# Low parts of 36 weight tiles made ahead, in the feed-forward stage, and kept in DRAM

## The chip, the cores and the metric

The kernel runs on one NeuronCore of a Trainium2 chip. The metric is the device time of one execution in microseconds, as the median of several runs. The engines go by short names: PE (TensorE matmul) and PEld (its weight loads), DVE (VectorE), ACT (ScalarE), POOL (GpSimd) and SP (SyncE, which here only issues DMAs).

## What is computed

Two transformer blocks in float32 on 512 tokens of 1024 features. The first has two mixers (a gated linear attention and a sliding-window attention) and a feed-forward part of 4096 hidden features. The second takes a vector `c` that modulates its norms, has two more mixers, and ends in a layer of 16384 single-neuron experts. What the change touches:

```python
# block 1, feed-forward
h = h + square(relu(f @ w_ff1)) @ w_ff2
# block 2, modulation
mod = silu(c) @ ada_w + ada_b                  # 6 x 1024 numbers
# block 2, experts, per token and head: the 16 best of 16384
s  = q @ sub_keys ; si = top_k(s, 16) ; eidx = si[0] * 128 + si[1]
act = gelu(x . u_tab[eidx]) ; y = sum(softmax(score) * act * v_tab[eidx])
```

## The kernel before, in words

**Products in two parts.** Every large product takes its float32 operands as a high part, rounded to the format in which PE is fast, and a low part, the rest. `split` (from line 287) makes both: ACT copies the high part, DVE or POOL subtracts it from the source. `chain` (line 327) then does three products per step: high x high (line 331), high x low (line 332) and, after all of these, low x high (line 334); the low part of the weights is needed last.

**Feed-forward stage (`ffn`, line 994).** Two halves of the hidden features (q = 0, 1). In each, 16 blocks of the first product, each ended by `ev` (relu on ACT, square on POOL, split on ACT and DVE), and then 16 steps of the second product. Weights come as 512 KB blocks on SP into four buffers (`weights`, line 296). Between these steps the generator `modulation` (line 501) is advanced: once per block of the first product, and 2 - q times per step of the second. A step of it issues the load of a 384 KB row block of `ada_w` on SP two steps ahead (line 523, three buffers) and adds one block to a sum on DVE (line 536). Every eighth step ends a sum: a transpose and a reduction on DVE (lines 542, 544) give `ap`, a small product on PE (line 546) adds over the partitions, and four small additions on DVE (`biased`, line 509) follow four steps later, once step KL = 3 of the next sum is through.

**The experts.** The first 128 tokens gather their experts' rows. For the other 384 tokens the first product is computed densely: 128 tiles of 128 experts each (`dense_S`, line 1570). A tile loads `ur` (512 KB, SP), makes `uh` (ACT, line 1575) and `ul` (line 1576), runs one chain of 24 matmuls, and applies gelu on ACT. `ur`, `uh` and `ul` have two buffers each. The first NSW = 59 tiles are made ahead of the second product, by `more_S`, while the routing runs; for these POOL makes `ul`, for the other 69 DVE does. The tiles beyond the sixth wait in DRAM (`Sd`).

**The routing** picks the experts. `topk_head` (line 1373) is a run of small DVE ops per head and token tile; `route_end` (line 1633) has PE transpose the numbers `ef`; `make` (line 1601) writes one-hot rows with DVE (`oh`, line 1612, and `ow`, line 1615, four buffers each), and `build` (line 1618) turns them into weights with PE (`gps`, line 1626). Per 16 tokens one `make`, one `topk_head` for the next tile, one `build` and 3, 2 or 1.5 tiles of `more_S` (for token tile 1, 2, 3) are written in this order.

**Order.** A planner orders each engine's instructions ahead of time, by the written order as priority and its own estimate of when operands are ready; each engine and each DMA queue then works through its list in order. `pin` puts an instruction behind the one written just before it on the same engine.

Of the kernel before, what the change touches and what calls it, by code (L numbers as in the profile page):

```python
# [9 lines left out]
F32 = mybir.dt.float32  # L10
# [11 lines left out]
KC = 8  # L22
# [13 lines left out]
NSW = 59  # L36
GBUF = 6
# [62 lines left out]
def layout(a):  # L100
    """the inputs in the order in which the kernel reads them: feature-major activations, weights in blocks of 128
    or 256 columns, one column per 128 entries of a vector"""
# [44 lines left out]
def tile_blocks(  # L147
# [26 lines left out]
    # ---------------------------------------------------------------- constants  # L174
# [72 lines left out]
    def small_constants():  # L247
        nc.scalar.dma_start(out=cf, in_=a["cf"])
        with tc.tile_pool(name="init", bufs=1) as ip:
# [4 lines left out]
            # sqrt(w^2 + eps) of the first block's last norm  # L254
# [28 lines left out]
    # ---------------------------------------------------------------- matrix products  # L283
# [12 lines left out]
    def weights(w, m, n, eng=None, step=None):  # L296
        """a block [128, m, n] of weights and its split, step of the m at a time"""
        if ready:
            return ready.pop(0)
        if raws:  # L300
            raw, step = raws.pop(0), W0
        else:
            raw = wtile(F32, "raw", RB, m, n)
            nc.sync.dma_start(out=raw, in_=w)
        hi = wtile(F32R, "whi", WB, m, n)
        lo = wtile(F32R, "wlo", WB, m, n)
        for k in range(0, m, step or m):
            ks = slice(k, k + (step or m))
            split(hi[:, ks], lo[:, ks], raw[:, ks], eng)
        return hi, lo, raw  # L310

    def ahead(w, hi, lo, eng=None, step=None):
        """a block of 128 columns split ahead of its turn, in other room than that of the weights"""
# [13 lines left out]
    def chain(ps, ab, first=True, last=True):  # L327
        """sum of a^T b over the pairs of split operands (a, b); a's low parts are needed last"""
# [7 lines left out]
    def gemm_fm(ws, X, N, evac, kouter=None, after=None, mid=None, eng=lambda s: None):  # L336
        """feature-major: evac(s, psum[128, N]) per block s of 128 columns; the first two blocks step by step together
        where kouter, the kind of their banks (their operand X is just coming in); after(s, raw weights);
        mid(k) after step k of these; eng(s): which engine makes the low parts of the weights"""
# [23 lines left out]
    def meta_fm(raw, um):  # L363
        """feature-major projection of the 16 meta tokens: psum[128, 16]"""
        ps = tr_tile("meta")
        for k in range(KC):
            PE.matmul(ps[:, 0:META], raw[:, k, :], um[:, k, :], start=(k == 0), stop=(k == KC - 1))
        return ps[:, 0:META]

    def gemm_tm(w, X, evac, after=None, n=256):  # L370
        """token-major: evac(b, psum[128 tokens, n]) for the n columns of w [128, KC, n]; one b per step"""
# [16 lines left out]
    def newton(ps, eps, n):  # L388
        """ps [128, n]: sums of D squares; -2 D / sqrt(ps / D + eps), its logarithm's estimate refined once"""
# [10 lines left out]
    def newton_small(ss, eps, n, tmp):  # L400
        """ss [128, m] SBUF: sums of n squares -> 1 / sqrt(ss / n + eps) in ss"""
# [8 lines left out]
    class SquareSum:  # L410
        """sums over the features of (x * wcol)^2: all chunks but the last are added up on the way"""
# [34 lines left out]
    def scaled_X(xr, wcol):  # L446
        """split of xr * wcol"""
# [5 lines left out]
    class Early:  # L453
        """two blocks of weights times X that still lacks the factor and the shift of its norm: flush(s) adds what the
        shift brings and evacuates"""
        def __init__(self, ws, X, cols, shift, evac, room, factor):
            """shift [128, KC]; room(s): two tiles of half a block's size; factor() makes the norm's factor"""
# [26 lines left out]
    def norm_X(X, xr, rs, wcol, bcol, keep=None):  # L484
        """split of xr * rs * wcol + bcol (wcol carries the factor of rs)"""
# [15 lines left out]
    def modulation(ip):  # L501
        """one step per call of next: rows of ada_w"""
# [6 lines left out]
        def biased(n, pm):  # L509
            o = VEC["ada_b_2"][0] + n * NM  # L510
            for e in range(4):
                es = slice(32 * e, 32 * e + 32)
                V.tensor_add(mod[es, n * NM:(n + 1) * NM], pm[es, 0:AW // 32].rearrange("p (m e) -> p m e", e=4)[:, :, e],
                             vec[es, o:o + NM])

# [12 lines left out]
        for n in range(6 * D // AW):  # L528
            am = ip.tile([128, AW], F32, name="am")
            for k in range(KC):  # L530
# [6 lines left out]
                if late and k == KL:  # L537
                    biased(*late.pop())
                yield
            # the sum over the partitions: 32 at a time by a transpose, the four of them by a product  # L540
# [4 lines left out]
            pm = tr_tile()  # L545
            PE.matmul(pm[:, 0:AW // 32], same32, ap, start=True, stop=True)
            late.append((n, pm))
        while late:
            biased(*late.pop())
# [8 lines left out]
    # ---------------------------------------------------------------- block 1  # L558
# [13 lines left out]
    def sigmoid(dst, src):  # L572
        """exp(-ln(1 + exp(-src))), src at least -43"""
# [4 lines left out]
    def gla(X, um, Y, sp, rs, rsT, hooks):  # L578
        """returns the parts in the order in which they may run; rs, rsT: factors of the columns and rows of products
        with X"""  # L580
# [35 lines left out]
        def decay():  # L616
            # decay: running sums of log sigmoid, restarted every 128 tokens
# [15 lines left out]
        def proj_v(h):  # L633
            """the values; with the first half of their columns, the 16 of the decay's first product"""
# [27 lines left out]
        def state():  # L662
            # state after the meta tokens
# [21 lines left out]
        def proj_r(i):  # L685
            """the gate of head i, into what it gates or in its place"""
# [17 lines left out]
        def within():  # L704
            """within a chunk: A^T[j, i], level by level, two chunks at a time; a level's factors are made a step ahead of its
            products"""
# [6 lines left out]
            def factors(n):  # L713
# [16 lines left out]
                # queries of the two heads of a pair side by side, each with zeros for the other's features  # L730
# [96 lines left out]
    def head_norm(po, eps, sp, rz=None):  # L827
        """token-major [128, 4 x 128] in PSUM -> rms normalised per head; rz: [128, 4] factors on po"""
# [17 lines left out]
    def swa(X, um, Y, sp, rs):  # L846
# [8 lines left out]
        # the rotated halves; all other rows stay zero  # L855
# [16 lines left out]
        def keys(ps, n, c0, rs=None):  # L872
            """the two kv heads, each then repeated on the other half of the partitions"""
# [89 lines left out]
    def out_proj(w, Yf):  # L963
        """half(kh, evac, pool): adds the products with half the rows of w, 256 columns per step"""
# [29 lines left out]
    def ffn(X, xr, rs, factor, step, done):  # L994
        """two halves of the hidden features: the first product's half stays on chip for the second; rs: the square
        of the factor of X's columns, made by factor()"""
        FH = DFF // NQ
        NS = FH // 128
        with stage("ffn") as sp:
            for q in range(NQ):  # L1000
                hh = sp.tile([128, NS, T], F32R, name="hh")
                hl = sp.tile([128, NS, T], F32R, name="hl")
                def ev(i, ps):
# [7 lines left out]
                    next(step)  # L1011
                gemm_fm(wrange(a["w_ff1"], q * NS, NS), X, T, ev, kouter="mm")
                for n2 in range(4):
                    pss = [bank("acc" if n2 % 2 else "sc", f"ff{e}") for e in range(2)]
                    for kq in range(NS // 4):
                        r0 = q * NS + kq * 4
                        for _ in range(2 - q):
                            next(step)
                        hi, lo, _ = weights(a["w_ff2"][n2, :, r0:r0 + 4, :], 4, 256)
# [17 lines left out]
    def block1():  # L1037
# [69 lines left out]
        with tc.tile_pool(name="ada", bufs=2) as ip:  # L1107
            step = modulation(ip)
            ffn(X, xr, rs2, factor, step, done)
# [3 lines left out]
    # ---------------------------------------------------------------- block 2  # L1113
    def mlstm(X, Y, sp, sums, wb):
# [4 lines left out]
        # gates  # L1119
# [137 lines left out]
    def diff(X, Y, sp, gates):  # L1257
        """gates(b, psum[128 tokens, 8]): the gates of the other mixer come with the first values"""
# [65 lines left out]
    def block2(xr, X, wb, sums):  # L1324
        """sums: what gives the factor of the final norm of the first block times that of the first norm here; X comes in
        without it and without the shift"""
# [38 lines left out]
    # ---------------------------------------------------------------- experts  # L1365
# [7 lines left out]
    def topk_head(h, s, sp, ef, fv):  # L1373
        """s [128, 2, 128]: scores of the two halves of head h -> expert numbers (float) and scores of its 16 best"""
# [7 lines left out]
        # sums of the ranks a, b: a, b >= 4 has 24 sums before it that are no less, so only a < 4 (at 16 a + b) and b < 4  # L1382
        # (at 4 a + 48 + b) are wanted
# [50 lines left out]
    with stage("h2") as sp:  # L1434
        xts = [sp.tile([128, D], F32, name=f"xt{b}") for b in range(NB)]

        def rows_of(dst, src, h, copy):
            """the 4 chunks h of src [128, KC, 128 tokens], token-major"""
# [34 lines left out]
    # ---------------------------------------------------------------- gathered tokens (the first 128)  # L1473
# [38 lines left out]
    # until the second product starts, the room for its operands takes gathered rows  # L1512
# [18 lines left out]
    def gather_step(n=1.0):  # L1531
        """issue the next n gathers; their use follows GLAG gathers later"""
# [9 lines left out]
    # ---------------------------------------------------------------- dense tokens: first product  # L1542
# [7 lines left out]
    def more_S(n):  # L1550
        """n further tiles ahead of the second product; those beyond LA wait in DRAM"""
# [18 lines left out]
    def dense_S(i, eng, tag, bufs):  # L1570
# [5 lines left out]
        eng.tensor_tensor(out=ul, in0=ur, in1=uh.bitcast(F32), op=OP.subtract)  # L1576
# [6 lines left out]
    # ---------------------------------------------------------------- routing; weight of every expert per dense token  # L1583
# [14 lines left out]
    with tc.tile_pool(name="rt", bufs=1) as sp:  # L1598
        made = []

        def make(b, n):
            """one-hot rows of the two halves of the expert number for 16 tokens n of tile b, one of them times the
            score in two parts of 12 bits (times GS: far from the least numbers of 16 bits)"""
# [14 lines left out]
        def build(b, n):  # L1618
            """the weights of 16 tokens n of tile b"""
# [106 lines left out]
    # ---------------------------------------------------------------- residual, last norm, out  # L1726
# [10 lines left out]
    def rows():  # L1737
        """the last norm's weight and the gate of the residual, the same row on all partitions"""
# [34 lines left out]
    # ---------------------------------------------------------------- dense tokens: second product  # L1773
# [8 lines left out]
    def load_G(k, p):  # L1782
        """part p of GP of the weights of 8 tiles"""
# [11 lines left out]
    for i in range(128):  # L1795
# [21 lines left out]
        # the last NL tiles together: the first tokens are complete while the others are still being added  # L1817
# [48 lines left out]
```

## Time and profile before

| what | value |
|---|---|
| median of 3 runs | 2322.53 us (2321.42 to 2325.12) |
| span of the profiled execution | 2316.9 us (its own time is not listed apart; the runs lie 4.5 to 8.2 us above the span) |
| PE busy | 2196.2 us, 95% |
| DVE busy | 1781.6 us, 77% |
| POOL busy | 1031.0 us, 44% |
| ACT busy | 903.7 us, 39% |

A busy share is an average over stages; the feed-forward stage lies between some 278 and 640 us, the routing between some 944 and 1436 us. "Granted clock" is PE's, as a share of full speed. An entry such as `ul<-ur,uh` names what an instruction writes and reads; L1576 is line 1576 of the kernel.

### The profile page before, as it was taken

What the parts mean: (1) busy time and instruction counts of PE and PEld (TensorE: products, weight loads), DVE (VectorE), ACT (ScalarE), POOL (GpSimd) and SP (SyncE); (2) the same over time, 40 slices, a digit from 0 to 9 for tenths busy, and PEclk for the clock granted to TensorE, in tenths of its full rate; (3) what the DMA queues carried; (4) which work ended last, traced back from release to release, by engine and by line L of the source; (5) the groups of instructions that cost most, each with busy time, mean ns of one, the idle gap of its engine ahead of it and who ended that gap; (6) DMA issues with size and microseconds to landing.
All of it is one profiled execution on the core that took longest, in us unless ns stands there. A gap on an engine that the chain in (4) does not pass through costs nothing.

```text
span 2316.9 us, 30890 instructions
## 1 busy us (share of the span) xinstructions
PE 2196.2 (95%) x11067; PEld 1865.7 (81%) x11067; DVE 1781.6 (77%) x3276; ACT 903.7 (39%) x1529; POOL 1031.0 (44%) x609
## 2 busy tenths in 40 slices
PE   9999999999989999997979999999999999999996
PEld 7777777877768777776969998776789999999994
DVE  5876657654485787899999965565679998989987
ACT  3345542233334664533334443333333333333333
POOL 1310221121150003512334434777788787778776
PEclk9999999999999999998989999999999999999998
DMA  5111357553222212631545667888889999999983
GB/s 178 59 39 46 118 161 244 179 168 106 81 92 78 64 61 85 227 98 62 186 135 189 212 222 238 285 264 281 273 316 327 338 336 322 340 339 330 340 305 136
DMA packets 181268, 455.09 MB, mean 196 GB/s; under 512 B 16597, under 2 KB 82006, under 8 KB 178042
## 3 DMA queue, kind: packets, MB, share of 16 engines
q1 hardware_dynamic: 82080, 252.58, 32.7%
q0 software_dynamic: 36864, 134.23, 16.2%
q10 hardware_dynamic: 62170, 66.30, 8.3%
q8 instruction: 87, 1.43, 0.3%
q14 instruction: 67, 0.55, 0.1%
HBM read 412.63 MB, written 39.79 MB: 195 GB/s over the span
## 4 chain that ended last, share of the span: by engine, by line
PE 42%; DVE 25%; issue 16%; POOL 9%; DMA 5%; ACT 2%; ACTq 0%; POOLq 0%; DVEq 0%; SPq 0%
PE do L1826 6%; POOL gt L1484 5%; PE mm L331 4%; PE mm L332 3%; PE mm L334 3%; POOL vl L1807 3%; PE S L331 3%; PE S L332 3%; PE S L334 3%; DVE oh L1612 3%; PE ff L331 2%; PE ff L334 2%; PE ff L332 2%; DVE ow L1615 2%; DVE vacc L1510 1%
## 5 line engine op out<-in xcount | busy, mean ns | idle before, releaser
L331 PE MATMUL S<-xhi,uh 128*128 128x384 f32 x1024 | 355.8, 347 | 5.9 <-ACT sg L1580 4.7
L332 PE MATMUL S<-xlo,uh 128*128 128x384 f32 x1024 | 352.4, 344 | 0.0
L1576 POOL TENSOR_TENSOR ul<-ur,uh 128x1024 fp32r<-128x1024 f32 x59 | 157.7, 2677 | 289.8 <-ACT uh L1575 208.6
L289 DVE TENSOR_TENSOR wlo<-raw,whi 128x1024 fp32r<-128x1024 f32 (+4 forms) x150 | 175.6, 1175 | 129.9 <-ACT whi L288 100.4
L1826 PE MATMUL do<-vh,wl 128*128 128x512 f32 x768 | 245.7, 399 | 15.2 <-DVE wl L1814 15.1
L1826 PE MATMUL do<-vl,wh 128*128 128x512 f32 x768 | 245.9, 400 | 10.9 <-POOL vl L1807 10.7
L1826 PE MATMUL do<-vh,wh 128*128 128x512 f32 x768 | 245.9, 400 | 1.1 <-ACT vh L1806 0.9
L1510 DVE SCALAR_TENSOR_TENSOR vacc<-gt,act,vacc 128x1024 f32<-128x1024 f32 x127 | 211.0, 1661 | 41.9 <-DMA gt<-in_v_dram,eidx 40.2
L288 ACT CAST whi<-raw 128x1024 fp32r<-128x1024 f32 (+4 forms) x152 | 146.1, 969 | 231.9 <-PE ff L332 107.2
L1492 DVE SCALAR_TENSOR_TENSOR gt<-gt,h2t 128x1024 f32<-128x1024 f32 x118 | 176.4, 1503 | 65.3 <-DMA gt<-in_u_dram,eidx 65.1
L331 PE MATMUL mm<-xhi,whi 128*128 128x512 f32 x544 | 219.8, 404 | 0.7 <-DVE xc L1127 0.7
L1575 ACT CAST uh<-ur 128x1024 fp32r<-128x1024 f32 x128 | 134.4, 1050 | 215.5 <-DMA ur<-in_ut_dram 115.0
L332 PE MATMUL mm<-xlo,whi 128*128 128x512 f32 x544 | 217.2, 399 | 0.0
L1807 POOL TENSOR_TENSOR vl<-vr,vh 128x1024 fp32r<-128x1024 f32 x64 | 174.8, 2732 | 80.7 <-ACT vh L1806 72.7
L331 PEld LDWEIGHTS S<-xhi,uh 128*128 128x128 f32 x1024 | 199.0, 194 | 9.5 <-ACT sg L1580 5.0
L332 PEld LDWEIGHTS S<-xlo,uh 128*128 128x128 f32 x1024 | 198.8, 194 | 3.2
L334 PE MATMUL S<-xhi,ul 128*128 128x384 f32 x1024 | 201.1, 339 | 0.0
L1807 POOL TENSOR_TENSOR vl<-vx,vh 128x1024 fp32r<-128x1024 f32 x64 | 169.3, 2645 | 61.5 <-ACT vh L1806 60.7
L1813 ACT CAST wh<-sg 128x384 fp32r<-128x384 f32 x128 | 65.5, 513 | 316.9 <-PE do L1826 210.1
L1826 PEld LDWEIGHTS do<-vh,wl 128*128 128x128 f32 x768 | 145.1, 190 | 53.6 <-DVE wl L1814 20.7
L1826 PEld LDWEIGHTS do<-vl,wh 128*128 128x128 f32 x768 | 145.7, 191 | 50.8 <-POOL vl L1807 17.0
L1484 POOL DMA_INDIRECT gt<-in_v_dram,eidx x128 | 166.7, 1303 | 32.5 <-issue 25.4
(481 smaller groups left out, 4819.8 us busy)
## 6 DMA issues: line engine op xcount, KB each, us to landing
ur<-in_ut_dram SPq DMA_DIRECT2D x128, 512.0 KB, 5.5
raw<-in_w_ff_dram SPq DMA_DIRECT2D x64, 512.0 KB, 3.6
vr<-in_v_dram SPq DMA_DIRECT2D x64, 512.0 KB, 4.6
vx<-in_v_dram SPq DMA_DIRECT2D x64, 512.0 KB, 7.6
aw<-in_ada_w_dram SPq DMA_DIRECT2D x64, 384.0 KB, 3.8
Gd<-gst ACTq DMA_DIRECT2D x24, 1024.0 KB, 4.3
gti<-Gd ACTq DMA_DIRECT2D x90, 256.0 KB, 5.0
raw<-in_w_in_dram SPq DMA_DIRECT2D x32, 512.0 KB, 4.4
```

Of the source, the lines that this page charges most:

```text
L288: S.copy(hi, src)
L289: (eng or V).tensor_tensor(out=lo, in0=src, in1=hi.bitcast(F32), op=OP.subtract)
L331: PE.matmul(ps, ah, bh, start=first and i == 0, stop=False, skip_group_check=True)
L332: PE.matmul(ps, ah, bl, start=False, stop=False, skip_group_check=True)
L334: PE.matmul(ps, al, bh, start=False, stop=last and i == n - 1, skip_group_check=True)
L1484: pin(G.indirect_dma_start(out=gt, out_offset=None, in_=tab, in_offset=bass.IndirectOffsetOnAxis(ap=eidx[:, s:s + 1], axis=0)))
L1492: ins = V.scalar_tensor_tensor(gt, gt, 1.0, h2t, op0=OP.mult, op1=OP.mult, accum_out=act[:, s:s + 1])
L1510: V.scalar_tensor_tensor(vacc, gt, act[:, s:s + 1], vacc, op0=OP.mult, op1=OP.add)
L1575: S.copy(uh, ur)
L1576: eng.tensor_tensor(out=ul, in0=ur, in1=uh.bitcast(F32), op=OP.subtract)
L1807: G.tensor_tensor(out=vl, in0=vr, in1=vh.bitcast(F32), op=OP.subtract)
L1826: PE.matmul(po[2 * tb + h], w[:, ts], v[:, h * 512:(h + 1) * 512], start=first and n == 0, stop=last and n == 127, skip_group_check=True)
```

## The change

In the feed-forward stage a second generator, `low_parts`, is advanced once per block of the first product and once per step of the second, 64 times in all. It works on the first 36 tiles of U: it loads a tile on SP, two calls later makes the high part on ACT and overwrites the tile with its low part on DVE, and one call after that stores it to a new DRAM tensor `Ud` on ACT's queue. Three tiles start in every five calls; three of the four slots of a room of 16 KB per partition (that of the mixers' output `Y`, free by then) hold tiles, the fourth the high part. `dense_S` then loads the low part of these tiles from `Ud` on SP instead of subtracting on POOL. The high part is still made there, by ACT. In `modulation` the small product on PE is issued at step 3 of the next sum, and the additions that use it at step 5.

```diff
+NU = 36
+    Ud = spill.tile([NU, 128, KC, 128], F32, name="Ud")
...
+        def summed(n, ap):
+            pm = tr_tile()
+            PE.matmul(pm[:, 0:AW // 32], same32, ap, start=True, stop=True)
+            return n, pm
...
                 if late and k == KL:
+                    late.append(summed(*late.pop()))
+                if late and k == KL + 2:
                     biased(*late.pop())
                 yield
...
-            pm = tr_tile()
-            PE.matmul(pm[:, 0:AW // 32], same32, ap, start=True, stop=True)
-            late.append((n, pm))
+            late.append((n, ap))
         while late:
-            biased(*late.pop())
+            biased(*summed(*late.pop()))
...
+    def low_parts(room):
+        hi = room[:, 3, :].bitcast(F32R)
+        at = {}
+        for n in range(NU):
+            e = n // 3 * 5 + n % 3
+            for d, what in ((0, "load"), (2, "split"), (3, "store")):
+                at.setdefault(e + d, []).append((what, n))
+        for e in range(max(at) + 1):
+            for what, n in sorted(at.get(e, []), key=lambda w: ("store", "load", "split").index(w[0])):
+                t = room[:, n % 3, :]
+                if what == "load":
+                    pin(nc.sync.dma_start(out=t, in_=a["ut"][n].rearrange("p k e -> p (k e)")))
+                elif what == "split":
+                    S.copy(hi, t)
+                    V.tensor_tensor(out=t.bitcast(F32R), in0=t, in1=hi.bitcast(F32), op=OP.subtract)
+                else:
+                    pin(nc.scalar.dma_start(out=Ud[n].rearrange("p k e -> p (k e)"), in_=t))
+            yield
+        while True:
+            yield
...
-    def ffn(X, xr, rs, factor, step, done):
+    def ffn(X, xr, rs, factor, step, low, done):
...
                     next(step)
+                    next(low)
                 gemm_fm(wrange(a["w_ff1"], q * NS, NS), X, T, ev, kouter="mm")
...
                         for _ in range(2 - q):
                             next(step)
+                        next(low)
                         hi, lo, _ = weights(a["w_ff2"][n2, :, r0:r0 + 4, :], 4, 256)
...
-            ffn(X, xr, rs2, factor, step, done)
+            low = low_parts(p1.tile([128, 4, 1024], F32, tag="y", name="low"))
+            ffn(X, xr, rs2, factor, step, low, done)
...
         S.copy(uh, ur)
-        eng.tensor_tensor(out=ul, in0=ur, in1=uh.bitcast(F32), op=OP.subtract)
+        if i < NU:
+            nc.sync.dma_start(out=ul.bitcast(F32), in_=Ud[i])
+        else:
+            eng.tensor_tensor(out=ul, in0=ur, in1=uh.bitcast(F32), op=OP.subtract)
```

## Rows read from the trace of the kernel before

**Rows 1.** The page: span, and busy time, share and instructions of each engine
```profile
span 2316.9 us, 30890 instructions
PE 2196.2 (95%) x11067; PEld 1865.7 (81%) x11067; DVE 1781.6 (77%) x3276; ACT 903.7 (39%) x1529; POOL 1031.0 (44%) x609
```

**Rows 2.** Busy time by stretch: window, length, engines (instructions), granted clock, DMA share, GB/s
```profile
986.00:1334.00 348.00, 307.44 (x1805) 289.34 (x1806) 342.50 (x1203) 131.69 (x204) 118.20 (x46) 0.92 0.43 149
1099.00:1216.00 117.00, 99.99 (x616) 95.05 (x616) 116.96 (x357) 40.98 (x64) 43.11 (x16) 0.89 0.45 158
...
1324.00:1436.00 112.00, 106.75 (x681) 104.61 (x682) 74.41 (x96) 46.55 (x71) 41.77 (x17) 0.95 0.67 230
...
1856.00:1914.00 58.00, 58.00 (x293) 52.44 (x292) 52.97 (x57) 16.98 (x23) 49.22 (x29) 1.00 0.97 346
```

**Rows 3.** Waits of PE, 940 to 1450 us: us in total, times, longest
```profile
PE tr L1647 <- DVE ef L1407: 25.2, 2, 13.2
PE gps L1626 <- DVE ow L1615: 12.7, 10, 2.5
```

**Rows 4.** Tile `ul`, POOL: count, duration min/median/max in ns, first and last start
```profile
L1576 POOL TENSOR_TENSOR ul<-ur,uh x59: 2350/2411/6040, 951.5 to 1427.8; 128x1024 fp32r<-128x1024 f32 x59
```

**Rows 5.** Lines 1612 and 1402, DVE: count, duration min/median/max in ns
```profile
L1612 DVE TENSOR_TENSOR oh<-io,tT x96: 666/683/2902, 1101.1 to 1410.2; 128x1024 f16<-128x1024 f16 x96
...
L1402 DVE TENSOR_TENSOR oh<-af,iob x32: 666/684/3375, 957.5 to 1311.2; 128x512 bf16<-128x512 bf16 x32
```

**Rows 6.** Timeline of POOL and DVE: start, us (x2: two in a row)
```profile
951.54 4.77 POOL L1576 TENSOR_TENSOR ul<-ur,uh 128x1024 fp32r<-128x1024 f32 x2 [21.58 <-DMA ur<-in_ut_dram]
954.16 2.18 DVE L1397 SCALAR_TENSOR_TENSOR af<-ai 128x16 bf16<-128x16 uint32 x1
...
1266.16 6.51 POOL L1576 TENSOR_TENSOR ul<-ur,uh 128x1024 fp32r<-128x1024 f32 x2 [6.92 <-ACT uh L1575]
1267.88 2.40 DVE L1381 CAST sif<-si 128x32 bf16<-128x32 uint32 x1
```

**Rows 7.** Busy time by stretch, feed-forward stage, second product of the first half
```profile
378.80:390.00 11.20, 11.20 (x50) 9.06 (x50) 10.57 (x16) 2.10 (x2) 2.57 (x2) 1.00 0.76 248
390.00:401.20 11.20, 11.20 (x49) 9.01 (x48) 9.95 (x13) 2.11 (x2) 0.00 (x0) 1.00 0.87 293
```

**Rows 8.** Timeline of ACT and DVE, feed-forward stage, first product
```profile
304.50 1.06 ACT L288 CAST whi<-raw 128x1024 fp32r<-128x1024 f32 x1 [0.90 <-PE mm L332]
310.10 1.05 ACT L288 CAST whi<-raw 128x1024 fp32r<-128x1024 f32 x1 [0.90 <-PE mm L332]
...
306.42 1.23 DVE L289 TENSOR_TENSOR wlo<-raw,whi 128x1024 fp32r<-128x1024 f32 x1 [1.17 <-ACT whi L288]
```

**Rows 9.** DMA, 370 to 460 us: total; issues with size and median us to landing
```profile
DMA packets 6709, 20.45 MB, mean 227 GB/s; under 512 B 752, under 2 KB 752, under 8 KB 6704
...
aw<-in_ada_w_dram SPq DMA_DIRECT2D x30, 384.0 KB, 3.8
raw<-in_w_ff_dram SPq DMA_DIRECT2D x15, 512.0 KB, 3.6
```

**Rows 10.** Waits of PE, 250 to 660 us
```profile
PE tr L546 <- DVE ap L544: 4.1, 4, 1.1
```

**Rows 11.** Timeline of PE: one chain of a tile of U and the next one's start
```profile
1079.96 0.34 PE L331 MATMUL S<-xhi,uh 128*128 128x384 f32 x1
...
1082.73 1.55 PE L334 MATMUL S<-xhi,ul 128*128 128x384 f32 x8
1084.12 0.34 PE L331 MATMUL S<-xhi,uh 128*128 128x384 f32 x1
```

**Rows 12.** DMA, 944 to 1334 us: total; issues with size and median us to landing
```profile
DMA packets 20119, 61.92 MB, mean 159 GB/s; under 512 B 2093, under 2 KB 9261, under 8 KB 18070
...
ur<-in_ut_dram SPq DMA_DIRECT2D x46, 512.0 KB, 4.0
...
vx<-in_v_dram SPq DMA_DIRECT2D x2, 512.0 KB, 9.7
```

## The prediction

> **What bounds the kernel now.** I read the page first. TensorE (PE) is busy 95% of a 2316.9 us span [rows 1], but that share mixes stages with different limits, so next I asked for busy time by stretch [rows 2]. In the routing stretch, 986 to 1334 us, DVE is busy 342.5 of 348 us and PE 307.4: there DVE is the bound, PE has 40.6 us to spare and runs at a granted clock of 0.92. In 1099 to 1216 DVE is busy for all of the 117 us and PE for 100. After 1324 it turns round: DVE 74 of 112, PE 107.
>
> Then who keeps PE waiting there [rows 3]: 25.2 us in two transposes at the end of a tile's routing (they wait for the expert numbers `ef`) and 12.7 us before the products of the one-hot rows. All 37.9 us are waits for DVE.
>
> Then what keeps DVE so long. Line 1612 takes 0.683 us at the median and up to 2.90; line 1402 0.684 and up to 3.38 [rows 5]. The long ones lie beside the low parts of U that POOL makes, 59 of them at a median of 2.41 us [rows 4]. In the timeline an op on 16 elements takes 2.18 us and a cast of 32 elements 2.40 us, each while POOL has a `ul` in hand [rows 6]; these are the first and the last of 33 such DVE ops beside the first 36 `ul`. So a POOL subtract off the critical path costs the engine that sets the pace some two microseconds each.
>
> The Trainium skill has the reason (SBUF — State Buffer, section "Who interferes with whom"): VectorE and GpSimd share a port pair, and of two instructions that want it the second waits until the first is through. The trace agrees: 2.18 and 2.40 us beside a POOL op of some 2.4 [rows 6].
>
> In the feed-forward stage it is PE that sets the pace: 11.20 of 11.20 us busy in the stretches shown, with DVE at 10.57 and 9.95 and ACT at 2.1 [rows 7].
>
> **The change, part by part.**
>
> *Removed: 36 of 59 POOL subtracts.* All 36 start between 951 and 1270 us. Over their medians the 33 ops beside them take 60 us more. The bounds: an op that always came right behind POOL's start would wait for all of it, 36 x 2.41 = 87 us; one that comes half-way, 36 x 1.2 = 43. I take 60, the count itself. (By the skill's rule alone a held op could lose the whole 2.41 us; with 87 us freed the time would move to the upper end of the gain, 2267 below.) DVE then needs 342.5 - 60 = 283 us in a stretch for which PE needs 307. PE becomes the bound, and the gain is what PE waits for DVE, not what DVE saves. Of PE's waits I take the 25.2 us of the transposes whole and half of the 12.7 us (23 subtracts stay on POOL, and the last third of the stretch keeps its holds): 31.5 us. A mean clock of 0.92 means that 16% of 348 us, 56 us, ran at 1.2 GHz instead of 2.4, and much of that lies in and just behind the two long idle stretches; with them gone I take 5 us (bounds: 0, and 12 if the 25 us of it that aren't idle all double in speed). Together -36.5. Lower end of the gain: 10; upper: all 40.6 us and 12.
>
> *Added there: 36 loads of 512 KB on SP.* A load of `ul` waits until PE has ended the chain of two tiles before (two buffers). Behind it on SP stand the next tile's `ur`, the query weights and `skT`; for those ACT's `uh` and PE wait. A chain takes 4.16 us from its start to the next one's, and its low products start 2.77 us in [rows 11], so a load has 4.16 + 2.77 = 6.9 us even where tiles follow each other at once. The same size lands in 4.0 us at the median here, and 9.7 is the worst group [rows 12]. 36 x 0.524 = 18.9 MB more beside 61.9 MB raises the mean from 159 to some 210 GB/s. Bounds: 0, and 36 x 2.8 = 100 us if each landed in 9.7 with back-to-back tiles; near the median, I take +3.
>
> *Added in the feed-forward stage: 36 casts on ACT and 36 subtracts on DVE.* By the weights' own split of the same size, 1.05 us and 1.23 us [rows 8]: 38 us of ACT, 44 us of DVE, three in five steps of 5.60 us, so 0.63 and 0.74 us per step. What hides them is the PE chain that fills each step; without that cover DVE's 44 us would show. DVE has room over the stage, little in 378 to 401 us, where a wait of one or two steps for the modulation is made up before the low parts of the weights are due (last in their chain). I cost them at nothing by themselves.
>
> *Added: 36 loads on SP, 36 stores on ACT.* Each step gains three fifths of a load and a store of 0.524 MB each, 0.63 MB in 5.6 us, 112 GB/s. In the second product of the first half the two queues carry 227 GB/s already [rows 9], which makes 339; the most that a stretch shown moved is 346, at a DMA share of 0.97 [rows 2]. So these 16 steps run at the edge. A load waits for the store of three tiles before, and behind it on SP stand modulation rows and weights; a store waits for its subtract, and behind it on ACT stand `rl` and the casts, for which PE's banks and next block wait, with most of a step to spare. Bounds: 0; and if transfers held at the 293 GB/s and 0.87 of [rows 7], 339/293 of 90 us, +14. I take +3, near the lower end: 339 fits in 346 on the mean, but not where the planner bunches the rows (293 + 112 = 405).
>
> The Trainium skill speaks against the change here (DMA: Bandwidth & Descriptors, section "Issuing engines are not separate DMA queues"): transfers of ACT's queue take the same 16 engines. Were that not so, only the loads' half would count, 283 GB/s, and the term would be 0.
>
> *Moved: the modulation's small product.* It waits for DVE's `ap` with PE's queue behind it: 4.1 us in four waits [rows 10]. Four steps later `ap` is long done. The last of the eight still comes at once, at the end of the generator, so three waits of 1.0 us go: -3. The four small adds that follow come two steps later, ahead of the first use of `mod`; no cost.
>
> **Sum:** -36.5 + 3 + 3 - 3 = -33.5 on a span of 2316.9: 2283.4. The median of the runs, 2322.5, lies 5.6 us above the profiled span (all three runs lie 4.5 to 8.2 above it); I keep the 5.6: **2289 us**.
>
> **The rivals.**
>
> *Late loads take POOL's place.* For it: double buffers, one queue, and a landing of 9.7 us in the very stretch [rows 12]. Against it: 36 tiles over 320 us are one in 9 us, so most loads have more than the 6.9 us. With a third of them late by 2.8 us, 12 x 2.8 = 34 us: 2323, no change.
>
> *Slower: modulation rows come late in the feed-forward stage.* Two per step and three buffers: a row is asked for when the op of three before is done, so it has 3 x 2.8 - 1.0 = 7.4 us, and lands in 3.8 [rows 9]. DVE takes its queue in order, so a late row holds the weights' low parts and then PE. If loads beside the new traffic took 9.7 us, 32 rows x 2.3 = 74 us: 2289 + 74 = 2363. It decides from a lateness of 34/32 = 1.0 us, a landing of 8.4. Against it: 339 is below 346, and the rows' deadline is loose.
>
> *It doesn't do what it says:* the order that the planner picks puts the remaining 23 subtracts beside the same DVE ops, or something else holds them; then about 2322. 33 matches beside 36 subtracts speak against it, so 5%.
>
> *More than forecast:* all of PE's 40.6 us and the clock's 12 come back: 2322.5 - 56 = 2267.
>
> **How the numbers follow.** Forecast 72% (2275 to 2308), late loads 8%, slower 7%, no effect 5%, more 8%. The range takes in the forecast, "more", and late loads as far as a gain of 10 us: 2266 to 2312. About 0.2%, 4.6 us, is what a measurement of this kernel can tell from no change. Faster by over that: 72 + 8 + half of late loads, 84%; the same 7%; slower 9%.
>
> **What would show it.** Right: between 986 and 1334 the long forms of lines 1612 and 1402 thin out, the waits of the transposes for `ef` shrink from 25 us to under 5, PE nears 100% there, granted clock over 0.96, and the stretch is some 35 us shorter; DVE shows room. In the feed-forward stage PE stays gapless, but for one wait at the eighth small product. Wrong: PE waits for DMA `ul` or ACT `uh` in the routing, or for `whi`/`wlo` between 370 and 460 us with DVE waiting for `aw`; or long DVE forms that stay with no POOL subtract beside them.

## The result, and the profile after

The changed kernel takes 2289.98 us (median of 4 runs, 2286.63 to 2297.70) beside 2323.82 us for the kernel before in the same runs: ratio 0.986, 95% interval 0.9834 to 0.9886. The forecast was 2289. The total came out. What it was added up from did not: the routing gave some 12 us more, the feed-forward stage lost 15 us that were not forecast, and the two errors nearly cancel. The trace shows that at once.

The page of the kernel after:

```profile
span 2285.6 us, 31115 instructions
...
PE 2190.0 (96%) x11067; PEld 1858.7 (81%) x11067; DVE 1751.1 (77%) x3312; ACT 936.4 (41%) x1565; POOL 936.3 (41%) x573
```

POOL has 95 us less to do, ACT 33 more and DVE 30 less in sum. Where the time went is told by stage, cut at the same events in both traces: first relu and last product of the feed-forward stage, first product with U, first product with V. Busy time by stretch (columns as in [rows 2]), the kernel before:

```profile
275.40:632.50 357.10, 352.98 (x1516) 282.70 (x1515) 205.29 (x246) 116.20 (x149) 61.72 (x45) 1.00 0.52 159
632.50:951.50 319.00, 304.70 (x1574) 238.91 (x1572) 237.21 (x513) 172.10 (x381) 58.57 (x50) 0.99 0.26 84
951.50:1435.80 484.30, 435.37 (x2585) 409.87 (x2586) 442.35 (x1393) 190.70 (x296) 187.92 (x79) 0.94 0.49 170
1435.80:2316.90 881.10, 840.33 (x3978) 726.70 (x3976) 710.96 (x719) 302.69 (x421) 673.58 (x377) 0.98 0.86 302
```

and the kernel after:

```profile
277.10:647.50 370.40, 357.56 (x1516) 285.41 (x1516) 251.84 (x281) 147.20 (x184) 65.74 (x45) 0.99 0.74 254
647.50:967.40 319.90, 305.33 (x1575) 239.22 (x1574) 236.82 (x511) 172.30 (x382) 58.57 (x50) 0.99 0.26 84
967.40:1406.20 438.80, 423.96 (x2585) 400.70 (x2586) 382.70 (x1395) 191.07 (x296) 88.63 (x43) 0.98 0.67 231
1406.20:2285.60 879.40, 840.51 (x3978) 727.45 (x3976) 689.26 (x719) 303.32 (x421) 672.75 (x377) 0.98 0.86 302
```

The feed-forward stage starts 1.7 us later and is 13.3 us longer; the routing is 45.5 us shorter; the other two stages change by +0.9 and -1.7. Together -31.3 us of span. (A trace is one execution: the last stage, which no run here edits, takes 876.3 to 887.7 us in twelve of the thirteen traces and 899.4 in that of `ffn_only`, so a difference of a few us in it tells nothing.)

**Routing.** Who keeps PE waiting now, 940 to 1450 us (to be read beside [rows 3]):

```profile
PE gps L1663 <- DVE ow L1652: 6.3, 3, 2.5
PE tr L1684 <- DVE ef L1441: 6.0, 1, 6.0
...
PE S L336 <- DMA ul<-Ud: 0.9, 1, 0.9
```

37.9 us of waits for DVE have become 12.3, and the loads that replace POOL cost PE one wait of 0.9 us. PE's idle time in the stretch falls from 484.3 - 435.4 = 48.9 to 438.8 - 424.0 = 14.8 us. Its busy time falls by 11.4 us for the same 2585 matmuls, as the granted clock rises from 0.94 to 0.98.

**Feed-forward stage.** Waits of ACT and of DVE for the new work, 280 to 660 us:

```profile
ACT low L581 <- DMA low<-in_ut_dram: 75.2, 24, 8.7
```

```profile
DVE low L582 <- ACT low L581: 39.3, 21, 4.8
```

and of PE, 250 to 690 us:

```profile
PE tr L520 <- DVE ap L553: 8.5, 2, 5.7
...
PE mm L326 <- DVE wlo L291: 1.7, 1, 1.7
PE ff L336 <- DVE wlo L291: 1.6, 2, 1.3
...
PE mm L333 <- ACT rl L1038: 1.1, 1, 1.1
```

The longest of these waits of PE, 5.7 us for `ap`, in the timeline of the kernel after. ACT:

```profile
361.93 0.33 ACTq L584 DMA_DIRECT2D Ud<-low  x1
369.27 1.04 ACT L581 CAST low<-low 128x1024 fp32r<-128x1024 f32 x1 [6.72 <-DMA low<-in_ut_dram]
370.22 1.04 ACT L290 CAST whi<-raw 128x1024 fp32r<-128x1024 f32 x1
```

DVE:

```profile
364.54 0.98 DVE L551 STREAM_TRANSPOSE at<-am 128x768 f32<-128x768 f32 x1
370.35 1.23 DVE L582 TENSOR_TENSOR low<-low 128x1024 fp32r<-128x1024 f32 x1 [4.83 <-ACT low L581]
371.49 0.94 DVE L553 TENSOR_REDUCE ap<-at 128x24 f32<-128x768 f32 x1
```

and PE:

```profile
372.49 0.62 PE L520 MATMUL tr<-ap,same 128*128 128x24 f32 x2 [5.73 <-DVE ap L553]
```

The load of this tile was issued at 361.4 and its cast began at 369.3. Its subtract stands in DVE's list between the transpose and the reduction of a sum; held at its written place (experiment 4) it comes behind that reduction, four of the modulation's steps later. The cast of this tile stands at the same place in ACT's list in both, behind the last `hh` of the first product; the casts that fall into a first product stand two blocks or more earlier here than held. That fits a planner that took the data as landed sooner than it was; its estimate is not in the trace. ACT stands still for 6.7 us, DVE for 4.8 with the reduction to `ap` queued behind the low part, and PE, whose small product waits for `ap`, for 5.7.

The waits are not the whole loss. PE's idle time in the stage grows by 8.7 us (370.4 - 357.6 beside 357.1 - 353.0) and its busy time by 4.6 for the same 1516 matmuls. Behind each of the two waits for `ap`, of 5.7 and 2.8 us, the granted clock is at 0.50 for a while. Busy time by stretch, the kernel after:

```profile
371.50:378.30 6.80, 5.81 (x15) 4.65 (x16) 6.22 (x11) 0.00 (x0) 0.00 (x0) 0.50 0.82 265
566.00:569.40 3.40, 3.40 (x10) 2.62 (x9) 0.62 (x4) 1.26 (x2) 0.00 (x0) 0.50 0.56 208
```

PE is busy for 5.8 + 3.4 = 9.2 us at 1.2 GHz there, which would be 4.6 at 2.4.

### The profile page after: what moved, and what is told of

It is laid out like the page before. It is cut to its first block, busy times and chain, and to the rows that moved or that the text cites. A ratio compares the mean times of both kernels' runs of the same rounds, so it can differ in the third digit from the quotient of the medians.

```text
span 2285.6 us, 31115 instructions
## 1 busy us (share of the span) xinstructions
PE 2190.0 (96%) x11067; PEld 1858.7 (81%) x11067; DVE 1751.1 (77%) x3312; ACT 936.4 (41%) x1565; POOL 936.3 (41%) x573
## 4 chain that ended last, share of the span: by engine, by line
PE 31%; DVE 15%; issue 15%; POOL 10%; DMA 7%; ACT 1%; SPq 0%; POOLq 0%; DVEq 0%; ACTq 0%
POOL gt L1518 5%; PE do L1863 5%; POOL vl L1844 4%; PE S L336 4%; PE S L333 3%; PE S L334 3%; PE gps L1663 3%; DMA gt<-in_v_dram,eidx 3%; PE mm L336 2%; PE mm L333 2%; PE mm L334 2%; DVE vacc L1544 1%; PE ff L336 1%; PE ff L333 1%; PE ff L334 1%
## 5 line engine op out<-in xcount | busy, mean ns | idle before, releaser
L333 PE MATMUL S<-xhi,uh 128*128 128x384 f32 x1024 | 350.1, 342 | 0.9 <-ACT uh L1609 0.9
L334 PE MATMUL S<-xlo,uh 128*128 128x384 f32 x1024 | 346.4, 338 | 0.0
L291 DVE TENSOR_TENSOR wlo<-raw,whi 128x1024 fp32r<-128x1024 f32 (+4 forms) x150 | 185.7, 1242 | 82.2 <-ACT whi L290 53.2
L334 PEld LDWEIGHTS S<-xlo,uh 128*128 128x128 f32 x1024 | 194.1, 190 | 3.2
L1518 POOL DMA_INDIRECT gt<-in_u_dram,eidx x122 | 165.1, 1353 | 54.3 <-DVE cand L1420 27.8
L1518 POOL DMA_INDIRECT gt<-in_v_dram,eidx x128 | 171.9, 1343 | 32.5 <-issue 26.3
```

What stands on the lines that cost most here:

```text
L291: (eng or V).tensor_tensor(out=lo, in0=src, in1=hi.bitcast(F32), op=OP.subtract)
L333: PE.matmul(ps, ah, bh, start=first and i == 0, stop=False, skip_group_check=True)
L334: PE.matmul(ps, ah, bl, start=False, stop=False, skip_group_check=True)
L1518: pin(G.indirect_dma_start(out=gt, out_offset=None, in_=tab, in_offset=bass.IndirectOffsetOnAxis(ap=eidx[:, s:s + 1], axis=0)))
```

## Experiments

Eleven runs. "The stage" is the feed-forward stage, and its loss is how much later than in the kernel before its last product ends (there 632.5 us; the changed kernel loses 15.0).

**1. The two halves apart.** First the stage's half alone:

```diff
-        if i < NU:
-            nc.sync.dma_start(out=ul.bitcast(F32), in_=Ud[i])
-        else:
-            eng.tensor_tensor(out=ul, ...)
+        eng.tensor_tensor(out=ul, in0=ur, in1=uh.bitcast(F32), op=OP.subtract)
```

> The low parts are made and stored in the feed-forward stage as in the changed kernel, and the modulation's product comes late, but the experts' tiles don't use them: POOL subtracts for all 59 tiles as before. Theory (the two halves of the change add up, with the feed-forward stage paying 15 us where I had forecast 0): about 2323.8 + 15 = 2339 us, the last product of the feed-forward stage some 15 us later than before, and the routing stretch from the first tile of U to the first second product 484 us as before. Rival (the 15 us come from the routing half reaching back, as through another order of the lists): 2324.

Measured: 2339.57 us beside 2321.29, ratio 1.0087 (1.0054 to 1.0119). The stage loses 17.9 us; the routing takes 484.5 us, as before. By itself this half makes the kernel slower.

Then the routing's half (the product's return to its old place left out of the cut):

```diff
-        for n in range(NU):
+        for n in range(3):
...
-            nc.sync.dma_start(out=ul.bitcast(F32), in_=Ud[i])
+            nc.sync.dma_start(out=ul.bitcast(F32), in_=Ud[i % 3])
```

> Leaves out the making of 33 of the 36 low parts, so that three of them are used in turn for 36 tiles, and keeps the modulation's product at its old place: only three casts, subtracts, loads and stores are left in the feed-forward stage, and POOL is relieved of its 36 subtracts. Theory (the two halves add up, 45.5 us gained in the routing): 2323.8 - 45.5 = 2278, the routing stretch near 439 us. Rival (the routing gains my forecast of 33.5, and the rest of the shortening is that it starts later and finds its inputs ready): 2290.

Measured: 2281.84, ratio 0.9834 (0.9795 to 0.9873). The routing takes 437.4 us, 46.9 less: the theory's size, not that of my forecast. What I had not expected is that three low parts alone cost the stage 6.3 us: its first relu comes 1.6 us later, PE then waits 3.0 us for a `rl` that stands in ACT's list behind two casts and 3.5 us of waits for their loads, and PE's busy time is 1.7 us longer.

**2. Is it the hold on DVE?** The changed kernel with POOL still subtracting, for nobody:

```diff
             nc.sync.dma_start(out=ul.bitcast(F32), in_=Ud[i])
+            eng.tensor_tensor(out=ur, in0=ur, in1=uh.bitcast(F32), op=OP.subtract)
```

> The changed kernel, with POOL still subtracting for the 36 tiles, though into the room of the loaded tile, and nobody uses the result. Theory (what the change removes is the hold that a POOL subtract puts on DVE): the gain of the routing goes although no instruction waits for the result, routing stretch near 484 us, time near 2290 + 45 = 2335, and the long forms of the one-hot lines are back at 2.5 to 2.9 us. Rival (what counts is that the low part comes from DRAM earlier than POOL could make it, and PE and ACT wait less for it): it stays near 2290.

Measured: 2340.05, ratio 1.0088 (1.0064 to 1.0112), 5 us above the theory's value; the stage loses 17.5 us here. Busy time by stretch, the routing of this kernel:

```profile
970.20:1455.10 484.90, 435.86 (x2585) 410.32 (x2586) 442.35 (x1396) 189.50 (x296) 192.85 (x79) 0.93 0.61 209
```

Its line of one-hot rows (busy us, mean ns of one, idle time before), first in the kernel after and then in this one:

```profile
L1649 DVE TENSOR_TENSOR oh<-io,tT 128x1024 f16<-128x1024 f16 x96 | 80.2, 857 | 34.0 <-PE gps L1663 33.8
L1650 DVE TENSOR_TENSOR oh<-io,tT 128x1024 f16<-128x1024 f16 x96 | 90.1, 965 | 22.2 <-PE gps L1664 22.2
```

The longest form does not tell them apart (2.90 us in the kernel after, 2.88 here), as 23 subtracts stay on POOL in the one and 59 run in the other; the mean does. PE's longest wait here:

```profile
PE tr L1685 <- DVE ef L1441: 24.7, 2, 13.2
```

The stretch is back at 484.9 us and DVE at the 442.35 of the kernel before, with every low part loaded from DRAM and no use made of what POOL computes. (The next load into the tile's room waits for POOL, as it did before the change; PE waits once for such a tile's cast, 0.7 us.) The low part's way to PE plays no part: it is POOL's instruction beside DVE's that costs the 45 us.

**3. The modulation's product alone**, in the kernel before (the diff of the change, without the rest):

> The kernel before with the modulation's small product moved, and nothing else. As forecast, three waits of 1.0 us go: 2323.8 - 3 = 2321. Rival (the planner puts the product early again, as it isn't pinned, so the waits stay): 2324, with four waits for ap in the feed-forward stage as before.

Measured: 2321.17 beside 2321.29, ratio 1.0005 (0.9987 to 1.0023): no difference in the time. In the stage, two of the four waits are left, 2.1 us, and it ends 2.2 us earlier. One of them is that of the eighth sum, as forecast. The other is that of the second: its product still comes right behind its sum, at 363.93 us, where the kernel before has it at 364.78, so the rival holds for this one product. A gain of the size that I gave it is inside the noise of the rest.

**4. Why the stage loses 15 us.** The cast and the subtract held at their written place:

```diff
-                    S.copy(hi, t)
-                    V.tensor_tensor(out=t.bitcast(F32R), in0=t, in1=hi.bitcast(F32), op=OP.subtract)
+                    pin(S.copy(hi, t))
+                    pin(V.tensor_tensor(out=t.bitcast(F32R), in0=t, in1=hi.bitcast(F32), op=OP.subtract))
```

> The changed kernel, with the cast and the subtract of the low parts held at the place where they are written, two calls behind the load (the planner had put the casts ahead, so that ACT waited 75 us for the loads in 24 waits and DVE 39 us for ACT). Theory W (the 15 us of the feed-forward stage are lists that stand still for loads that the planner takes as landed): those waits nearly go, the last product of the stage comes 8 to 13 us earlier than in the changed kernel, and the time is 2277 to 2282. Rival (the added 38 us of ACT and 44 us of DVE, or the DMA traffic, slow the stage by themselves): PE loses the same, 2287 to 2292.

Measured: 2279.43, ratio 0.9823 (0.9796 to 0.985). Busy time by stretch, the stage of this kernel, and then what PE waits for in it:

```profile
277.00:634.40 357.40, 352.96 (x1516) 282.38 (x1516) 249.01 (x282) 149.97 (x185) 66.40 (x45) 1.00 0.77 263
```

```profile
PE ff L336 <- DVE wlo L291: 2.5, 2, 1.7
PE tr L520 <- DVE ap L553: 1.9, 2, 1.0
```

With all 36 loads, casts, subtracts and stores still in it, at 263 GB/s and DVE at 249 us, the stage takes 357.4 us against 357.1 before; it loses 1.9 us in all, nearly all of it ahead of its first relu. ACT's waits for these loads fall from 75.2 to 7.8 us. So neither the work nor the traffic cost anything by itself; the order did.

The product three steps later instead, step 6 and additions at step 7:

```diff
-                if late and k == KL:
+                if late and k == KL + 3:
                     late.append(summed(*late.pop()))
-                if late and k == KL + 2:
+                if late and k == KL + 4:
```

> The changed kernel, with the modulation's small product three steps later still (step 6 of the next sum, the additions at step 7). In the changed kernel PE waits 8.5 us in two waits for ap there. If these waits are what the stage loses most by: 2290 - 8 = 2282. Rival (DVE's lateness is only met at another place, at the low parts of the weights): 2287 to 2290, with new PE waits for wlo.

Measured: 2288.87, ratio 0.9866 (0.9837 to 0.9896), the rival's value. Waits of PE in this kernel, 262 to 655 us:

```profile
PE ff L336 <- DVE wlo L291: 8.1, 4, 5.7
PE ff L333 <- ACT whi L290: 2.0, 3, 1.2
...
PE tr L520 <- DVE ap L553: 1.2, 1, 1.2
```

The wait for `ap` goes from 8.5 to 1.2 us, and that for the weights' low parts comes up to 8.1. The small product was only where PE first met a DVE that ran late.

Both edits together:

> Both of these: split held at its place, product at step 6. By theory W the feed-forward stage loses less than 3 us against the kernel before, and the time is 2321.3 - 45.5 + 0 to 3 = 2276 to 2279. Rival: above 2285.

Measured: 2281.54, ratio 0.982 (0.9797 to 0.9843). The time is neither in the theory's range nor in the rival's: the stage loses 5.7 us, with one wait of 4.4 us for `wlo`. The later product adds nothing to the held split.

And the loads left out, with the work kept:

```diff
                 if what == "load":
+                    if n < 3:
-                    pin(nc.sync.dma_start(out=t, ...))
+                        pin(nc.sync.dma_start(out=t, ...))
```

> The changed kernel without 33 of the 36 loads of the feed-forward stage: from the fourth tile on the split works on what lies in the room (so most of the low parts are those of other tiles), while all casts, subtracts and stores remain. Theory W: the stage loses 6 us or less of its 15, as in the kernel with three low parts alone: about 2281. Rival, the work on ACT and DVE itself: stays at 2290.

Measured: 2277.95, ratio 0.9806 (0.9767 to 0.9846); the stage loses 4.8 us, with the same 36 casts and subtracts. Ten of the 15 us go with the loads. It is not ACT's standing still as such that costs: its casts of low parts still wait 61.5 us here, 51.9 of them for a subtract on DVE. What has gone is DVE's wait for these casts, 3.6 us beside the 39.3 of the changed kernel; with the split held it is 3.4. But the lists are not those of the changed kernel (without loads the planner puts the splits earlier still), and DVE's subtracts now wait 24.0 us for stores, so this run by itself doesn't tell the loads' landing from the order.

**5. The better version again**, on one chip with the changed kernel, five runs of each:

> The changed kernel once more, beside the next two on one chip: 2290, as measured.

> The kernel with the split held at its place once more. If its gain of some 10 us over the changed kernel is real: 2277 to 2282, with an interval that lies below that of the changed kernel. If the one measurement flattered it: above 2285.

> The split held at its place, and the modulation's product back at its old place at the end of its sum. If the late product is worth the 2 us that the feed-forward stage showed when it was moved alone: 2281 to 2284, with PE waiting 4 to 8 us for ap. If it is worth more once DVE carries the low parts, as a DVE that runs late meets PE there: 2285 to 2292, with waits for ap of 10 us and more.

Measured, beside 2321.69 for the kernel before: the changed kernel 2288.14, ratio 0.9852 (0.9825 to 0.9879); split held at its place 2274.18, 0.979 (0.9761 to 0.982); the same with the product at its old place 2276.70, 0.9805 (0.9778 to 0.9832). The second interval lies below the first: holding two instructions is worth some 14 us, more than the 10 that I had expected (2274.18 is below my 2277 to 2282). The product's place can't be told apart by the time, and both values that I gave for the old one were too high. Both stages end at 633.9 us, with 4.9 us of waits for `ap` in five waits at the old place and 1.9 in two at the new one; from its first relu the stage takes 359.6 us at the old place and 357.4 at the new, the 2 us of the product moved alone. I had expected a late DVE to make more of it; with the split held, DVE waits only 3.4 us for these casts at either place.

## Why the prediction was right, and where it was wrong

*DVE freed, "60, the count itself".* Right: DVE's busy time in the routing falls from 442.35 to 382.70, 59.7 us.

*"PE becomes the bound, and the gain is what PE waits for DVE."* Right, and the run with the idle subtract shows that the hold is the cause of the routing's gain. Of the waits I took 31.5 us; PE's idle time fell by 34.1. The transposes' waits for `ef` fell to 6.0 us, not quite under the 5 that I gave as a sign.

*The clock, 5 us with a bound of 12.* Mis-sized: the same matmuls take 11.4 us less, near the bound. Worked out as in the prediction, the time at 1.2 GHz falls from 12% of 484.3 us to 4% of 438.8, so from some 58 us to some 18.

*Late `ul` loads, +3.* 0.9 us. The rival that was built on them did not come.

So the routing gave 45.5 us where the sum had 33.5, between the forecast and the rival *more than forecast* (whose 40.6 and 12 make 52.6; the prediction's 56 comes out only with the small product's 3 as well).

*Casts and subtracts in the feed-forward stage, "I cost them at nothing by themselves"; DMA, +3.* Wrong in sum: the stage lost 15 us. The step that failed is the list of waits that the change adds. I named the load's wait for a store and the store's wait for a subtract, but not the cast's wait for its load, and took "two calls later" in the source for the order on ACT and DVE. The planner moves what isn't pinned. The cover that I named, the PE chain, does hide the work (held at its place it costs nothing); it doesn't hide a DVE that stands behind such a cast, 39.3 us in 21 waits, nor what the clock takes after PE's own waits, 4.6 us. The slower rival had DVE waiting for modulation rows; those waits were 5.0 us in four, beside 3.8 in five before.

*The DMA's edge.* The mean of 339 GB/s that I forecast for the second product of the first half came out, at 338. Busy time by stretch, the kernel after:

```profile
370.00:460.00 90.00, 85.94 (x359) 68.65 (x360) 79.29 (x94) 26.47 (x28) 10.55 (x6) 0.96 0.94 338
390.00:448.00 58.00, 56.66 (x247) 45.40 (x246) 52.24 (x64) 16.52 (x16) 10.09 (x6) 1.00 0.98 359
```

The 346 that I took as the most, a mean over 58 us, is passed by little over as long a stretch, 359 at a DMA share of 0.98. Over shorter ones more went through. DMA, 380 to 475 us, of the kernel after (GB/s in 40 slices):

```profile
GB/s 273 219 257 202 402 417 388 343 293 339 307 294 291 303 422 416 417 409 414 305 326 308 323 303 414 418 406 356 354 340 373 395 379 401 321 38 74 147 0 0
```

Slices of 2.4 us reach 422; in the kernel before, slices of 2.25 us between 370 and 460 us reach 369. That this traffic is not what the stage lost by is shown by the held split, which moves 263 GB/s over the stage and takes no longer than before. The sentence of the Trainium skill that ACT's transfers take the same 16 engines (DMA: Bandwidth & Descriptors, section "Issuing engines are not separate DMA queues") isn't tested by that: loads and stores together found room.

*The small product, -3.* About 2 us alone, as the second sum's product stayed right behind its sum, and in the changed kernel the two waits that were left grew to 8.5.

The sum: -45.5 in the routing, 12 more than forecast; +15 in the feed-forward stage, 15 worse; -0.8 elsewhere. 2289 was hit by errors that cancelled, which was luck. Had the stage come out at 0, as forecast, the rest as measured would have given 2323.8 - 46.3 = 2278, and that is where the kernel stands once the split is held.

## What to carry to other kernels

Where DVE sets the pace and POOL has time, POOL work is not free: here each of 36 elementwise POOL subtracts (128x1024, 2.41 us) cost DVE 1.7 us on average (59.7 / 36), so it paid to make the result elsewhere, in a stage with another bound. When work is moved into a stage "with room", check every wait that it puts into an in-order queue, the consumer's wait for the load first, and hold the consumer behind it in the list; a distance written in the source is not a distance in the list. And a total that comes out proves no term: compare the stages.

## What the runs showed that was not expected

A small early start is dear: three low parts alone lost the stage 6.3 us, as their casts and loads fell among its first steps. A wait of PE costs more than itself: behind waits of 5.7 and 2.8 us the granted clock was 0.50 for 6.8 and 3.4 us. And the DMA engines moved up to 422 GB/s in slices of 2.4 us, where the slices that I had read in the kernel before reached 369.
